# Strassen's seven products in the second MLP matmul of a Griffin-style block

## The chip, the cores and the metric

One core of a Trainium2 chip runs the kernel. The metric is the device time of one execution in microseconds (us). Engines are named as the profile names them: PE is TensorE (PEld its weight loads), DVE is VectorE, ACT is ScalarE, POOL is GpSimd, SP is SyncE, whose queue (SPq) issues every DMA here.

## The reference

One hybrid decoder block on 512 positions of 1024 channels: a mixer (RG-LRU branch and differential attention, merged and projected) and then a channel part, which is where the change lies. Cut to that part:

```python
h2 = rms_norm(x) * (1.0 + scale2) + shift2          # 512 x 1024
ff = jnp.square(jax.nn.relu(h2 @ w_ff1[l])) @ w_ff2[l]   # 1024 -> 4096 -> 1024
x = x + gate2 * ff
```

`shift2`, `scale2`, `gate2` are three of the six modulation vectors `c_act @ w_ada + b_ada`.

## The kernel before

All is fp32. A product in full precision is made of three matmuls in the float32r type: each operand is split into a high part (a cast to float32r) and a low part (the remainder), and `mm3` adds high x high, high x low and low x high in PSUM. `load_w` brings a weight block of 128 x 1024 into one of three `w` buffers, ACT casts it to `wh` (two buffers), DVE subtracts to get `wl` (two buffers). `project` multiplies such a block with all eight 128-row chunks of an activation: 8 x 3 = 24 matmuls of 512 columns, which give 128 output channels by 512 positions; I call this a block.

The MLP goes over four quarters `qd` of the 4096 hidden channels. In each, eight blocks of the first product (`project(w_ff1[qd, n], h2)`, tiles `f`) are passed through relu (ACT), squared (DVE), and split into `rh` (ACT) and `rlo` (DVE). Then eight blocks of the second product run over the quarter's 1024 hidden channels, and DVE adds each, scaled by `gate2`, to the residual `x1[n]` (line 867). In quarter 0 one `ada_chunk(5, n)` stands behind each of these blocks: it loads 128 x 1024 of `w_ada` into a `w` buffer and DVE reduces it to a column of `gate2` (line 183). In the last block of all, the 512 positions are done as two halves of 256 columns, so that the first half's store runs beside the second half. The first two blocks of quarter 0 (`early`, tiles `f1e`) are computed ahead, from the activation that is not yet normalised.

What is queued on each engine is set by a scheduler at build time, which may move independent instructions past one another; `tc.high_priority` lets the weight splits go ahead. At run time every engine takes its instructions in that order.

```python
wh, wl = load_w(src)
for k in range(KC):
    c0 = slice(k * P, (k + 1) * P)
    mm3(ps, wh[:, c0], wl[:, c0], act[k][0], act[k][1], k == 0, k == KC - 1)
```

Of the kernel before, what the change touches and what calls it, by code (L numbers as in the profile page):

```python
# [42 lines left out]
HP = 130  # L43
# [10 lines left out]
def build(tc, out, x, xT_in, c, pos, vecs, reps, ada, w_xr, w_xr7, w_qk, w_v, w_gr, w_gm, w_lru,  # L54
          w_pr, w_pa, w_out, w_ff1, w_ff2):
    nc = tc.nc
    from contextlib import ExitStack

    with ExitStack() as es:
        const = es.enter_context(tc.tile_pool(name="const", bufs=1))  # L60
        wpool = es.enter_context(tc.tile_pool(name="w", bufs=3))
        big = es.enter_context(tc.tile_pool(name="big", bufs=1))
        tmp = es.enter_context(tc.tile_pool(name="tmp", bufs=1))
        psum = es.enter_context(tc.tile_pool(name="ps", bufs=1, space=bass.MemoryType.PSUM))

        B_Q, B_Y, B_M, B_H, B_V, B_T, B_A, B_R = 12, 24, 8, 16, 8, 4, 6, 5

        def slot(tag, bufs, name, dt=F32):
            return big.tile([P, S], dt, name=name, tag=tag, bufs=bufs)

        def t_(name, dt=F32, tag="t"):
            return tmp.tile([P, S], dt, name=name, tag=tag, bufs=dict(t=B_T, a=B_A, r=B_R)[tag])

        def tiny(name, n, dt=F32):
            return tmp.tile([P, n], dt, name=name, tag=f"s{n}", bufs=4 if n >= 32 else 12)
# [1 line left out]
        def bank(name, tag="mm", bufs=4, dt=F32):  # L77
            return psum.tile([P, S], dt, name=name, tag=tag, bufs=bufs)
# [25 lines left out]
        def f32(t):  # L104
            return t.bitcast(F32)
# [4 lines left out]
        def load_w(src, n=1024):  # L110
            u = n_unit[0]
            n_unit[0] += 1
            w = wpool.tile([P, 1024], F32, name=f"w{u}", tag="w", bufs=3)
            nc.sync.dma_start(w[:, :n], src)
            wh = wpool.tile([P, 1024], F32R, name=f"wh{u}", tag="wh", bufs=2)
            wl = wpool.tile([P, 1024], F32R, name=f"wl{u}", tag="wl", bufs=2)
            with tc.high_priority(HP):
                i_w = nc.scalar.copy(wh[:, :n], w[:, :n])  # L118
                nc.vector.tensor_tensor(wl[:, :n], w[:, :n], f32(wh)[:, :n], op=ALU.subtract)  # L119
            last_wh[0] = i_w  # L120
            return wh, wl

        def mm3(ps, lh, ll, rh, rl, first, last):
            nc.tensor.matmul(ps, lh, rh, start=first, stop=False)  # L124
            nc.tensor.matmul(ps, lh, rl, start=False, stop=False)  # L125
            nc.tensor.matmul(ps, ll, rh, start=False, stop=last)  # L126

        def project(src, act, name):

            wh, wl = load_w(src)  # L130
            ps = bank(name)
# [3 lines that stand above are left out]
            return ps  # L135

        def split_l(dst, src, h):
            return nc.vector.tensor_tensor(dst, src, f32(h), op=ALU.subtract)  # L138


        c_sb = [t_(f"c_sb{i}") for i in range(2)]
        for i in range(2):
            nc.sync.dma_start(c_sb[i][0:1, :], c[:, i * S:(i + 1) * S])
        xt = [[slot("y", B_Y, f"x{i}_{j}") for j in range(2)] for i in range(TB)]
        for i in range(TB):
            for j in range(2):
# [8 lines left out]
        ident = const.tile([P, P], F32, name="ident")  # L155
# [45 lines left out]
        def mcol(j, k):  # L201
            return mod[:, j * 8 + k:j * 8 + k + 1]
# [30 lines left out]
        def bcast_cols(src, name, *where):  # L233

            dg = t_(name + "d")
            nc.vector.tensor_tensor(dg.rearrange("p (a b) -> p a b", b=P),
                                    ident[:, None, :].to_broadcast([P, TB, P]),
                                    src[:, :, None].to_broadcast([P, TB, P]), op=ALU.mult)
            pb = bank(name, *where)
            nc.tensor.matmul(pb, ones, dg, start=True, stop=True)  # L240
            return pb
# [19 lines left out]
        h = []  # L261
# [28 lines left out]
            return w  # L290

        nxt = first_chunk(0)
        rep = tmp.tile([P, 6, 64], F32, name="rep", tag="a", bufs=B_A)
        nc.sync.dma_start(rep, reps)
        pos_i = const.tile([P, TB], I32, name="pos_i")
        nc.sync.dma_start(pos_i, pos)
        for k in range(KC):
            wh, wl = nxt
            if k + 1 < KC:
                nxt = first_chunk(k + 1)  # L300
            for n in range(NK):
                c0 = slice(n * P, (n + 1) * P)
# [3 lines left out]
        def vtiny(name, n=8):  # L306
            return const.tile([P, n], F32, name=name)
# [13 lines left out]
        pl = vtiny("sp_p")  # L321
# [11 lines left out]
        for i in range(2):  # L333
            lj = t_(f"lj{i}")[:, :64]
            i_ = nc.vector.tensor_tensor_reduce(lj, rep[:, 2 + 2 * i], rep[:, 3 + 2 * i], 1.0, 0.0,
                                                op0=ALU.mult, op1=ALU.add, accum_out=lam2[:, i:i + 1])
# [13 lines left out]
        R = [P, TB, 32]  # L350

        def rtile(name):
            return tmp.tile(R, F32, name=name, tag="a", bufs=B_A)

        fr = rtile("fr")
        for i in range(32):
# [3 lines left out]
        kk = rtile("kk")  # L360
# [393 lines left out]
        for n in range(KC):  # L754
# [5 lines left out]
            mh = slot("y", B_Y, f"mh{n}", F32R)  # L760
# [7 lines left out]
        x1, hu = [], []  # L768
        acc = t_("acc", tag="a")
        for n in range(KC):  # L770
# [3 lines left out]
            t = slot("m", B_M, f"x1_{n}")  # L774
# [22 lines left out]
        rs2 = tiny("rs2", 4)  # L797
        rsqrt(rs2, pss[:, 0:2 * TB:2], 4, 1.0 / D, EPS, "r2")
        rb2p = bcast_cols(rs2, "rb2", "sc", 2)
        rb2 = t_("rb2s", tag="a")  # L800
        nc.scalar.copy(rb2, rb2p)


        NU = 2
        early = []
        pcs = bank("shift2w", "o", 1)
        for n in range(NU):
            wh, wl = load_w(w_ff1[0, n])
# [9 lines left out]
        shw = const.tile([P, NU], F32, name="shw")  # L818
        nc.vector.tensor_reduce(shw, pcs[:, :2 * NU].rearrange("p (a b) -> p a b", b=2), axis=AX.X, op=ALU.add)

        h2 = []
        for k in range(KC):
            t = t_(f"h2f{k}")
# [5 lines left out]
            h2.append((hh, hl))  # L829


        for qd in range(4):
            r2_ = []
            for n in range(KC):
                rl = t_(f"rl{qd}_{n}")
                if qd == 0 and n < NU:
                    nc.vector.tensor_tensor(rl, early[n], rb2, op=ALU.mult)
                    nc.scalar.activation(rl, rl, AF.Relu, bias=shw[:, n:n + 1])
                else:
                    ps = project(w_ff1[qd, n], h2, f"f1_{qd}_{n}")  # L840
                    nc.scalar.activation(rl, ps, AF.Relu)
                nc.vector.tensor_tensor(rl, rl, rl, op=ALU.mult)
                i = 2 * n
                tags = [("y", B_Y)] * 2 if qd % 2 == 1 else [("q", B_Q) if i + j < 12 else ("v", B_V) for j in (0, 1)]
                rh = slot(*tags[0], f"rh{qd}_{n}", F32R)
                nc.scalar.copy(rh, rl)
                rlo = slot(*tags[1], f"rlo{qd}_{n}", F32R)
                split_l(rlo, rl, rh)
                r2_.append((rh, rlo))
            for n in range(KC):  # L850
                if qd == 3 and n == KC - 1:

                    wh, wl = load_w(w_ff2[qd, n])
                    for hf in range(2):
                        cols = slice(hf * 256, hf * 256 + 256)
                        ps = bank(f"f2_{qd}_{n}_{hf}")[:, :256]
                        for k in range(KC):
                            c0 = slice(k * P, (k + 1) * P)
                            mm3(ps, wh[:, c0], wl[:, c0], r2_[k][0][:, cols], r2_[k][1][:, cols], k == 0, k == KC - 1)
                        nc.vector.scalar_tensor_tensor(x1[n][:, cols], ps, mcol(5, n), x1[n][:, cols],  # L860
                                                       op0=ALU.mult, op1=ALU.add)
                        nc.sync.dma_start(out[n][:, cols], x1[n][:, cols])
                    continue
                ps = project(w_ff2[qd, n], r2_, f"f2_{qd}_{n}")
                if qd == 0:
                    ada_chunk(5, n)
                nc.vector.scalar_tensor_tensor(x1[n], ps, mcol(5, n), x1[n], op0=ALU.mult, op1=ALU.add)  # L867
                if qd == 3:
                    nc.sync.dma_start(out[n], x1[n])


# [64 lines left out]
```

## Time and profile before

| what | value |
|---|---|
| runs: median (lowest to highest) | 906.08 us (905.87 to 906.85) |
| the profiled execution: its time | 905.49 us |
| the profiled execution: its span, first to last instruction | 903.7 us |
| busy in the span: PE, DVE, ACT | 98%, 63%, 43% |
| mean granted TensorE clock | 0.999 |
| chain that ended last: PE, DVE, DMA | 78%, 12%, 4% |

The page tells for each engine how much of the span it was busy, in 40 slices how that was spread, and who waited for whom. Matmuls are pipelined, so a matmul's shown length is not the time that it takes from the next; the starts tell that. An engine that idles costs nothing as long as PE does not wait for it.

### The profile page before, as it was taken

Reading aid. Unit: us, or ns where it says so; the run is one execution under the profiler, and the core shown is the slowest. Engines: PE = TensorE matmul, PEld = TensorE weight load, DVE = VectorE, ACT = ScalarE, POOL = GpSimd, SP = SyncE. Lnnn points to the kernel's source line nnn. Section 1 sums busy time; section 2 is a strip of 40 time slices with the busy share of each in tenths; the row PEclk is TensorE's granted clock in tenths of the full one; section 3 lists DMA queues with packets and bytes.
Section 4 is the critical chain, followed back from the end, with each engine's and each line's share of the span. In section 5 each row is a group of like instructions: output and inputs, shape, how many; then the busy total and the mean of one; then the engine's idle time right before and its main releaser. Section 6 shows DMA issues by size and latency. Waiting matters only on the chain.

```text
span 903.7 us, 11146 instructions
## 1 busy us (share of the span) xinstructions
PE 883.1 (98%) x4076; PEld 720.1 (80%) x4076; DVE 570.8 (63%) x1144; ACT 390.1 (43%) x676; POOL 2.2 (0%) x40
## 2 busy tenths in 40 slices
PE   6999999999999999999999999999999999999998
PEld 3888887777878878787778888888888888888887
DVE  6963974599969775987867566865344334334442
ACT  6663545985446444435533343531242133223420
POOL 0000000000000000000000000000000000000000
PEclk9999999999999999999999999999999999999999
DMA  8943226222263673367546332355222223322241
GB/s 321 343 144 105 94 101 156 102 70 71 76 156 121 178 217 120 137 165 226 203 144 206 117 105 71 100 183 200 99 94 94 94 94 99 110 94 94 93 140 47
DMA packets 42154, 121.57 MB, mean 135 GB/s; under 512 B 5618, under 2 KB 6002, under 8 KB 42100
## 3 DMA queue, kind: packets, MB, share of 16 engines
q1 hardware_dynamic: 42100, 120.87, 41.8%
q8 instruction: 32, 0.52, 0.2%
q14 instruction: 22, 0.18, 0.1%
HBM read 106.17 MB, written 2.10 MB: 120 GB/s over the span
## 4 chain that ended last, share of the span: by engine, by line
PE 78%; DVE 12%; DMA 4%; ACT 2%; issue 2%; SPq 2%; ACTq 0%; DVEq 0%
PE f L126 12%; PE f L124 12%; PE f L125 12%; DMA ada<-in_ada 3%; DVE wl L119 3%; PE xr L124 2%; PE xr L126 2%; PE xr L125 2%; PE wo L126 2%; PE wo L124 2%; PE gr L126 2%; PE gr L124 2%; PE wo L125 2%; PE gr L125 2%; PE qk L126 2%
## 5 line engine op out<-in xcount | busy, mean ns | idle before, releaser
L118 ACT CAST wh<-w 128x1024 fp32r<-128x1024 f32 (+1 forms) x145 | 151.6, 1046 | 330.6 <-PE f L125 176.8
L119 DVE TENSOR_TENSOR wl<-w,wh 128x1024 fp32r<-128x1024 f32 (+1 forms) x145 | 176.3, 1216 | 114.6 <-ACT wh L118 110.1
L125 PE MATMUL f<-rlo,wh 128*128 128x512 f32 (+1 forms) x264 | 101.1, 383 | 0.0
L126 PE MATMUL f<-rh,wl 128*128 128x512 f32 (+1 forms) x264 | 101.0, 383 | 0.0
L124 PE MATMUL f<-rh,wh 128*128 128x512 f32 (+1 forms) x264 | 101.0, 383 | 0.0
L126 PE MATMUL f<-h2h,wl 128*128 128x512 f32 x240 | 93.3, 390 | 0.1
L124 PE MATMUL f<-h2h,wh 128*128 128x512 f32 x240 | 93.2, 390 | 0.0
L125 PE MATMUL f<-h2l,wh 128*128 128x512 f32 x240 | 92.7, 389 | 0.0
L867 DVE SCALAR_TENSOR_TENSOR x<-f,mod,x 128x512 f32<-128x512 f32 x31 | 23.3, 751 | 86.7 <-PE f L126 86.7
L125 PEld LDWEIGHTS f<-rlo,wh 128*128 128x128 f32 x264 | 49.6, 188 | 10.0 <-DVE rlo L138 0.3
L124 PEld LDWEIGHTS f<-rh,wh 128*128 128x128 f32 x264 | 49.6, 188 | 9.7
L126 PEld LDWEIGHTS f<-rh,wl 128*128 128x128 f32 x264 | 49.6, 188 | 9.7
L126 PEld LDWEIGHTS f<-h2h,wl 128*128 128x128 f32 x240 | 45.0, 188 | 10.0 <-DVE wl L119 0.6
L183 DVE CUSTOM_DVE_ANT_0 ada<-ada,cb,bada 128x1024 f32<-128x1024 f32 x32 | 41.0, 1282 | 18.9 <-DMA ada<-in_ada 18.7
L125 PEld LDWEIGHTS f<-h2l,wh 128*128 128x128 f32 x240 | 45.0, 188 | 9.4
L124 PEld LDWEIGHTS f<-h2h,wh 128*128 128x128 f32 x240 | 45.1, 188 | 9.2
L126 PE MATMUL gm<-hh,wl 128*128 128x512 f32 x128 | 51.0, 399 | 0.0
L124 PE MATMUL gm<-hh,wh 128*128 128x512 f32 x128 | 50.8, 397 | 0.0
L124 PE MATMUL qk<-wh,hh 128*128 128x512 f32 x128 | 50.7, 398 | 0.0
L125 PE MATMUL gm<-hl,wh 128*128 128x512 f32 x128 | 50.7, 396 | 0.0
L126 PE MATMUL qk<-wh,hl 128*128 128x512 f32 x128 | 50.6, 395 | 0.0
L125 PE MATMUL qk<-wl,hh 128*128 128x512 f32 x128 | 50.3, 393 | 0.0
(314 smaller groups left out, 1734.8 us busy)
## 6 DMA issues: line engine op xcount, KB each, us to landing
w<-in_w_ff SPq DMA_DIRECT2D x64, 512.0 KB, 3.2
ada<-in_ada SPq DMA_DIRECT2D x32, 512.0 KB, 4.3
ada<-in_ada SPq DMA_DIRECT2D x32, 256.0 KB, 5.8
w<-in_w_qk SPq DMA_DIRECT2D x16, 512.0 KB, 3.3
w<-in_w_gm SPq DMA_DIRECT2D x16, 512.0 KB, 3.7
w<-in_w_gr SPq DMA_DIRECT2D x8, 512.0 KB, 3.3
w<-in_w_v SPq DMA_DIRECT2D x8, 512.0 KB, 3.2
kh<-qh SPq DMA_DIRECT2D x32, 128.0 KB, 2.4
```

The lines of the kernel that those rows point to most:

```text
L118: i_w = nc.scalar.copy(wh[:, :n], w[:, :n])
L119: nc.vector.tensor_tensor(wl[:, :n], w[:, :n], f32(wh)[:, :n], op=ALU.subtract)
L124: nc.tensor.matmul(ps, lh, rh, start=first, stop=False)
L125: nc.tensor.matmul(ps, lh, rl, start=False, stop=False)
L126: nc.tensor.matmul(ps, ll, rh, start=False, stop=last)
L183: nc.vector.tensor_tensor_reduce(w, w, cb, 1.0, bada[:, col:col + 1], op0=ALU.mult, op1=ALU.add, accum_out=mod[:, col:col + 1])
L867: nc.vector.scalar_tensor_tensor(x1[n], ps, mcol(5, n), x1[n], op0=ALU.mult, op1=ALU.add)
```

## The change

The quarter's second product is written with the positions as rows: activations A (512 positions x 1024 hidden, cut in halves A11, A12, A21, A22) times weights B (1024 hidden x 1024 outputs, cut in halves), by Strassen's scheme in Winograd's form, seven products of halves in place of eight. One product of halves is 2 row tiles x 4 hidden chunks x 3 = 24 matmuls, with a split activation chunk as the stationary operand and 512 output channels as the moving one.

- The squared activations stay unsplit in `raw` (ACT squares, no longer DVE). Sums of halves of A are made on DVE in `sx`, and each operand is split just before its product (`split_a`).
- B is loaded in eight tiles per quarter (`b`, in pieces of 1 KB); DVE forms sums of B tiles in place (`sums`); each operand is cast and subtracted in two halves (`split_b`), with two buffers for each half.
- The seven products go p1, p5, p6, p3, p7, p2, p4 (in quarter 3: p1, p2, p5, p6, p3, p7, p4). They accumulate in PSUM banks X, Z and Y, and after each DVE adds the bank to C in SBUF (`add_c`; the first time ACT copies it).
- In quarters 0 to 2 three blocks of the next quarter's first product (`beside`) run before p1, after p5 and after p6.
- At the end, `finish` transposes C with 32 transposes on PE and DVE adds it to `x1`; the last product is computed the other way round, in 48 matmuls of 256 columns, and needs no transpose.
- The eight `ada_chunk(5, n)` of quarter 0 stand together behind the first product's eight blocks.
- The buffers of the mixer come from a pool `mix`, closed before the MLP, whose memory the pool `ff` takes over.

```diff
-            for n in range(KC):
-                rl = t_(f"rl{qd}_{n}")
...
-                nc.vector.tensor_tensor(rl, rl, rl, op=ALU.mult)
...
-                ps = project(w_ff2[qd, n], r2_, f"f2_{qd}_{n}")
-                if qd == 0:
-                    ada_chunk(5, n)
-                nc.vector.scalar_tensor_tensor(x1[n], ps, mcol(5, n), x1[n], op0=ALU.mult, op1=ALU.add)
...
+        mix_es.close()
+        ff = es.enter_context(tc.tile_pool(name="ff", bufs=1))
...
+                    for hf in range(2):
+                        b = ff.tile([P, 4, 2 * P], F32, name=f"b{qd}_{k}{c}{hf}", tag="b", bufs=8)
+                        k0 = (4 * k + 2 * hf) * P
+                        nc.sync.dma_start(b, w_ff2[qd, 4 * c:4 * c + 4, :, k0:k0 + 2 * P].rearrange("n p f -> p n f"))
...
+                with tc.high_priority(HP):
+                    nc.scalar.copy(v4(wh), v)
+                    nc.vector.tensor_tensor(v4(wl), v, f32(v4(wh)), op=ALU.subtract)
...
+                        nc.vector.tensor_tensor(dst, dst, ps[t], op=ALU.add if sign > 0 else ALU.subtract)
...
+                fs = [split_b(b, f"{name}_{qd}_{i}", i) for i, b in enumerate(bs)]
+                for hf in range(2):
+                    for t in range(2):
+                        for kk in range(2):
+                            k = 2 * hf + kk
+                            ts = slice(t * P, (t + 1) * P)
+                            mm3(ps[t], a[0][:, k, ts], a[1][:, k, ts], fs[hf][0][:, kk], fs[hf][1][:, kk],
+                                first and k == 0, k == 3, not first)
...
+            if qd == 3:
+                second()
+            b12 = get_b(0, 1)
+            sums(b11, b12)
+            Z = [bank(f"Z{qd}_{t}") for t in range(2)]
+            product("p5", s1, b11, Z, True)
+            beside()
+            with tc.high_priority(HP):
+                nc.vector.tensor_tensor(sx, sx, A[0][0], op=ALU.subtract)
+                s2 = split_a(sx, "s2")
+            add_c(1, 1, Z, 1)
+            b22 = get_b(1, 1)
+            sums(b11, b22)
+            product("p6", s2, b11, X, False)
+            beside()
...
+            raw = hidden(qd, ahead)
+            if qd == 0:
+                for n in range(KC):
+                    ada_chunk(5, n)
...
+            beside()
+            out_product(qd, raw, beside)
```

Where the instructions then stand, at two places. First DVE around the end of quarter 0's hidden blocks (`wl` is a weight subtraction, `ada` a reduction, `a11l`, `s1l` low parts of activations, `p_0_1l` the low part of p1's second weights). Before:

```order
L119 TENSOR_TENSOR wl_5764<-w_5761,wh_5763 128x1024
L842 TENSOR_TENSOR rl_6_5685<-rl_6_5685 128x512
L138 TENSOR_TENSOR rlo_6_5721<-rl_6_5685,rh_6_5719 128x512
L119 TENSOR_TENSOR wl_5799<-w_5796,wh_5798 128x1024
L842 TENSOR_TENSOR rl_7_5723<-rl_7_5723 128x512
L183 ISA ada_5862,mod<-ada_5862,cb,bada 128x1024
L183 ISA mod 128x1
L138 TENSOR_TENSOR rlo_7_5759<-rl_7_5723,rh_7_5757 128x512
L867 SCALAR_TENSOR_TENSOR x_0_5035<-f_0_0_5767,mod,x_0_5035 128x512
L119 TENSOR_TENSOR wl_5834<-w_5831,wh_5833 128x1024
```

Now:

```order
L188 ISA ada_5753,mod<-ada_5753,cb,bada 128x1024
L188 ISA mod 128x1
L188 ISA ada_5756,mod<-ada_5756,cb,bada 128x1024
L188 ISA mod 128x1
L188 ISA ada_5759,mod<-ada_5759,cb,bada 128x1024
L188 ISA mod 128x1
L957 TENSOR_TENSOR sx_5839<-r_0_0_5532,r_0_1_5533 128x512
L123 TENSOR_TENSOR wl_5766<-w_5763,wh_5765 128x1024
L905 TENSOR_TENSOR p_0_1l<-b_001_5799,p_0_1h 128x1024
L143 TENSOR_TENSOR s1l_5843<-sx_5839,s1h_5842 128x512
```

A reduction between two weight subtractions was one of a pair before; now the subtraction for the first block of quarter 1 (`wl_5766`) stands behind all eight reductions, and its load stands behind their loads on SP.

Then DVE in quarter 3, from the splits for p6 to the addition that frees Z for p3 (`p_3_0l`, `p_3_1l` low parts of weights, `s4l` of an activation sum, `C` the accumulators). Before, at this place of quarter 3:

```order
L119 TENSOR_TENSOR wl_7534<-w_7531,wh_7533 128x1024
L867 SCALAR_TENSOR_TENSOR x_1_5075<-f_3_1_7504,mod,x_1_5075 128x512
L119 TENSOR_TENSOR wl_7567<-w_7564,wh_7566 128x1024
L867 SCALAR_TENSOR_TENSOR x_2_5117<-f_3_2_7537,mod,x_2_5117 128x512
L119 TENSOR_TENSOR wl_7600<-w_7597,wh_7599 128x1024
```

Now:

```order
L905 TENSOR_TENSOR p_3_1l<-b_111_7643,p_3_1h 128x1024
L948 TENSOR_TENSOR b_000_7495<-b_000_7495,b_100_7556 128x1024
L948 TENSOR_TENSOR b_001_7497<-b_001_7497,b_101_7558 128x1024
L905 TENSOR_TENSOR p_3_0l<-b_010_7594,p_3_0h 128x1024
L918 TENSOR_TENSOR C_5524<-C_5524,Y_0_7554 128x512
L905 TENSOR_TENSOR p_3_1l<-b_011_7596,p_3_1h 128x1024
L918 TENSOR_TENSOR C_5525<-C_5525,Y_1_7555 128x512
L918 TENSOR_TENSOR C_5530<-C_5530,Z_0_7600 128x512
```

One subtraction and one addition per block have become a row of sums, splits and additions, with the additions that free Y and Z behind the splits for later products.

## Rows read from the trace of the kernel before

**Rows 1.** The page: busy time of each engine, then tenths in 40 slices.
```profile
PE 883.1 (98%) x4076; PEld 720.1 (80%) x4076; DVE 570.8 (63%) x1144; ACT 390.1 (43%) x676; POOL 2.2 (0%) x40
...
DVE  6963974599969775987867566865344334334442
```
**Rows 2.** Windows over quarter 1: stretch, length, busy time by engine, granted clock, DMA.
```profile
638.70:682.20 43.50, 43.50 (x193) 36.04 (x192) 19.62 (x23) 16.23 (x22) 0.00 (x0) 1.00 0.29 97
682.20:725.70 43.50, 43.50 (x193) 36.03 (x192) 16.36 (x17) 9.55 (x10) 0.00 (x0) 1.00 0.28 97
```
**Rows 3.** Timeline of PE at the end: start, duration, instruction.
```profile
889.17 0.39 PE L124 MATMUL f<-rh,wh 128*128 128x512 f32 x1
...
894.61 0.28 PE L124 MATMUL f<-rh,wh 128*128 128x256 f32 x1
894.72 0.28 PE L125 MATMUL f<-rlo,wh 128*128 128x256 f32 x1
...
900.24 0.28 PE L126 MATMUL f<-rh,wl 128*128 128x256 f32 x1
```
**Rows 4.** Waits: engine, line, for whom; us in total, times, longest.
```profile
ACT wh L118 <- PE f L125: 176.8, 57, 4.4
DVE wl L119 <- ACT wh L118: 110.1, 56, 4.6
```
**Rows 5.** Transposes on PE: timeline in the attention stage, and their group.
```profile
427.90 0.60 PE L598 MATMUL aT<-ident,e 128*128 128x128 f32 x4
428.25 0.48 PE L124 MATMUL gm<-hh,wh 128*128 128x512 f32 x1
428.57 0.39 PE L125 MATMUL gm<-hl,wh 128*128 128x512 f32 x1
...
L598 PE MATMUL aT<-ident,e 128*128 128x128 f32 x80 | 14.2, 276 | 2.2 <-DVE yal L640 1.8 <-DVE or0b L94 0.2
```
**Rows 6.** Timeline of DVE where operations follow each other without a gap.
```profile
563.16 1.23 DVE L119 TENSOR_TENSOR wl<-w,wh 128x1024 fp32r<-128x1024 f32 x1 [0.19 <-ACT wh L118]
564.30 0.75 DVE L828 SCALAR_TENSOR_TENSOR h2l<-h2f,mod,h2h 128x512 fp32r<-128x512 f32 x1
...
568.93 0.69 DVE L837 TENSOR_TENSOR rl<-f1e,rb2s 128x512 f32<-128x512 f32 x1
569.53 0.74 DVE L828 SCALAR_TENSOR_TENSOR h2l<-h2f,mod,h2h 128x512 fp32r<-128x512 f32 x1
```
**Rows 7.** Timeline at hidden block 4 of quarter 0 (ACT, DVE, PE).
```profile
571.38 1.05 ACT L118 CAST wh<-w 128x1024 fp32r<-128x1024 f32 x1 [0.94 <-PE f L125]
...
572.47 1.23 DVE L119 TENSOR_TENSOR wl<-w,wh 128x1024 fp32r<-128x1024 f32 x1 [0.99 <-ACT wh L118]
...
573.75 0.50 PE L126 MATMUL f<-h2h,wl 128*128 128x512 f32 x1
574.09 0.39 PE L124 MATMUL f<-h2h,wh 128*128 128x512 f32 x1
```
**Rows 8.** The tile `ada` in quarter 0: reductions (ns) and loads.
```profile
L183 DVE CUSTOM_DVE_ANT_0 ada<-ada,cb,bada x8: 1284/1285/1286, 584.4 to 625.7; 128x1024 f32<-128x1024 f32 x8
...
DMA to landing us min/median/max: 3.4/4.3/4.6
```
**Rows 9.** Timeline of DVE: the last read of PSUM.
```profile
900.56 0.48 DVE L860 SCALAR_TENSOR_TENSOR x<-f,mod,x 128x256 f32<-128x256 f32 x1 [2.39 <-PE f L126]
```
**Rows 10.** DMA from 14 to 38 us in 40 slices; then stores in 1 KB pieces.
```profile
GB/s 362 389 382 388 404 410 377 377 386 396 411 406 383 388 386 386 405 393 406 380 392 389 386 388 404 382 406 379 386 399 397 395 378 366 386 392 417 389 382 395
...
out_dram<-x SPq DMA_DIRECT2D x2, 128.0 KB, 1.7
```
**Rows 11.** A window with PE half idle, and PE's longest wait.
```profile
420.00:425.00 5.00, 2.92 (x18) 2.32 (x19) 4.34 (x9) 5.00 (x11) 0.00 (x0) 1.00 0.44 161
...
PEld warm L217 <- DMA x<-in_x: 6.3, 1, 6.3
```

More of the change, by code (lines that the diff above doesn't have):

```diff
@@ L64, in build @@
         psum = es.enter_context(tc.tile_pool(name="ps", bufs=1, space=bass.MemoryType.PSUM))
+        mix_es = ExitStack()
+        mix = mix_es.enter_context(tc.tile_pool(name="mix", bufs=1))
         B_Q, B_Y, B_M, B_H, B_V, B_T, B_A, B_R = 12, 24, 8, 16, 8, 4, 6, 5
         def slot(tag, bufs, name, dt=F32):
-            return big.tile([P, S], dt, name=name, tag=tag, bufs=bufs)
+            return (big if tag in "mh" else mix).tile([P, S], dt, name=name, tag=tag, bufs=bufs)
         def t_(name, dt=F32, tag="t"):
-            return tmp.tile([P, S], dt, name=name, tag=tag, bufs=dict(t=B_T, a=B_A, r=B_R)[tag])
+            return (tmp if tag == "t" else mix).tile([P, S], dt, name=name, tag=tag,
+                                                     bufs=dict(t=B_T, a=B_A, r=B_R)[tag])
         def tiny(name, n, dt=F32):
@@ L121, in load_w, with mm3 @@
             return wh, wl
[L123 to L126, printed above, removed]
+        def mm3(ps, lh, ll, rh, rl, first, last, more=False):
+            nc.tensor.matmul(ps, lh, rh, start=first, stop=False, skip_group_check=more)
+            nc.tensor.matmul(ps, lh, rl, start=False, stop=False, skip_group_check=more)
+            nc.tensor.matmul(ps, ll, rh, start=False, stop=last, skip_group_check=more)
         def project(src, act, name):
@@ L292, in build @@
         nxt = first_chunk(0)
-        rep = tmp.tile([P, 6, 64], F32, name="rep", tag="a", bufs=B_A)
+        rep = mix.tile([P, 6, 64], F32, name="rep", tag="a", bufs=B_A)
         nc.sync.dma_start(rep, reps)
@@ L352, in rtile @@
         def rtile(name):
-            return tmp.tile(R, F32, name=name, tag="a", bufs=B_A)
+            return mix.tile(R, F32, name=name, tag="a", bufs=B_A)
         fr = rtile("fr")
@@ L799, in build @@
         rb2p = bcast_cols(rs2, "rb2", "sc", 2)
-        rb2 = t_("rb2s", tag="a")
+        rb2 = t_("rb2s")
         nc.scalar.copy(rb2, rb2p)
@@ L829, in build @@
             h2.append((hh, hl))
-        for qd in range(4):
-            r2_ = []
-            for n in range(KC):
-                rl = t_(f"rl{qd}_{n}")
[L836 to L841, printed above, removed]
-                nc.vector.tensor_tensor(rl, rl, rl, op=ALU.mult)
[L843 to L863, printed above, removed]
-                ps = project(w_ff2[qd, n], r2_, f"f2_{qd}_{n}")
-                if qd == 0:
-                    ada_chunk(5, n)
-                nc.vector.scalar_tensor_tensor(x1[n], ps, mcol(5, n), x1[n], op0=ALU.mult, op1=ALU.add)
-                if qd == 3:
-                    nc.sync.dma_start(out[n], x1[n])
@@ new lines, in build, with hidden_relu @@
+        mix_es.close()
+        ff = es.enter_context(tc.tile_pool(name="ff", bufs=1))
+        C = [[[ff.tile([P, S], F32, name=f"C{r}{c}{t}", tag="c", bufs=8) for t in range(2)]
+              for c in range(2)] for r in range(2)]
+        H2 = S // 2
+        def hidden_relu(qd, n, dst):
+            if qd == 0 and n < NU:
+                nc.vector.tensor_tensor(dst, early[n], rb2, op=ALU.mult)
+                nc.scalar.activation(dst, dst, AF.Relu, bias=shw[:, n:n + 1])
+            else:
+                ps = project(w_ff1[qd, n], h2, f"f1_{qd}_{n}")
+                nc.scalar.activation(dst, ps, AF.Relu)
@@ new lines, in build, with finish @@
+        n_fin = [0]
+        def finish(n, t0, t1, store=True):
+            pt = bank(f"cT{n}_{t0}", *(("tp", 1), ("o", 1))[n_fin[0] % 2])
+            n_fin[0] += 1
+            for t in range(t0, t1):
+                nc.tensor.transpose(pt[:, t * P:(t + 1) * P], C[t // 2][n // 4][t % 2][:, n % 4 * P:(n % 4 + 1) * P],
+                                    ident)
+            cols = slice(t0 * P, t1 * P)
+            nc.vector.scalar_tensor_tensor(x1[n][:, cols], pt[:, cols], mcol(5, n), x1[n][:, cols],
+                                           op0=ALU.mult, op1=ALU.add)
+            if store:
+                nc.sync.dma_start(out[n][:, cols], x1[n][:, cols])
@@ L873, in layout, with beside @@
+        ahead = []
+        for qd in range(4):
+            raw = hidden(qd, ahead)
+            if qd == 0:
+                for n in range(KC):
+                    ada_chunk(5, n)
+            ahead = []
+            def beside():
+                if qd < 3:
+                    ahead.append(t_(f"ahead{qd + 1}_{len(ahead)}"))
+                    hidden_relu(qd + 1, len(ahead) - 1, ahead[-1])
+            beside()
+            out_product(qd, raw, beside)
 def layout(inputs):
```

103 lines of the change are left out of this document (added).

## The prediction

> **What bounds the kernel now.** I read the page's busy shares and its 40 slices first. TensorE (PE) is busy 98% of the span, VectorE (DVE) 63%, ScalarE (ACT) 43%, and DVE's digits fall to 3 and 4 in the last third, where the MLP runs [rows 1]. Next the windows over the MLP: in the first product of quarter 1 PE is busy 43.50 us of 43.50 and DVE 19.62, in its second 43.50 and 16.36 [rows 2]. So PE bounds the whole MLP, and the order of its matmuls in the timeline gives the price: 24 of them (one block) from 889.17 to 894.61, 5.44 us, which is 0.2267 us each; the last 48, of 256 columns, start 0.12 us apart [rows 3]. The 0.39 us shown for each is its whole passage; they overlap. DVE and ACT mostly wait for PE here, as the waits say: 176.8 us of ACT's weight casts behind PE, 110.1 us of DVE's subtractions behind ACT [rows 4]. Fewer matmuls are therefore time gained, as long as DVE, which takes over the sums, stays ahead.
>
> **PE's work.** Seven products of 24 matmuls replace eight blocks of 24 in each of four quarters: 4 x 24 = 96 fewer, x 0.2267 = **-21.8 us**. (The last product of all stays in 48 pieces of 256 columns, as the last block was.) Added are 32 transposes of C. The trace has such transposes in fours: four start at 427.90, the next matmul at 428.25 and the one after at 428.57, so four cost 0.35 + 0.32 - 0.23 = 0.44 us [rows 5], 0.11 each, **+3.5 us** for 32. Their mean duration is 276 ns [rows 5]. The Trainium skill (TensorE: Matmul & The Clock Gate, Part 4: PE-mode transpose) counts about 275 ns for one in a kernel's context; if that were the slot it takes, 32 would be +8.8 us. The trace agrees with that as a duration and not as a slot, so the 0.11 stands.
>
> **DVE's work.** Back to back, an operation of 1024 columns starts 1.14 us before the next (563.16 to 564.30), one of 512 with PSUM or SBUF 0.60 (568.93 to 569.53), though they last 1.23 and 0.69 [rows 6]. A quarter's products cost DVE 14 weight splits, 8 sums of weights, 7 splits and 4 sums of activations, 14 additions to C. Where two hidden blocks run among the products (quarters 0 to 2), I count in the order 26 wide and 15 half operations between the start of the first product and the end of the seventh: 26 x 1.14 + 15 x 0.60 = 38.6 us, beside 9 x 5.44 = 49.0 us of PE. The cover is thus PE itself. Walking the queue in order, the tightest place is the weight subtraction of the second block run among the products, done 1 to 2 us before PE wants it. So quarters 1 and 2 cost **0**, bounded by nothing and 2 us each (a cast and a subtraction late: 1.05 + 1.14 [rows 6, 7]). ACT takes the squares from DVE and stays under its share; nothing of it is on the path.
>
> **Quarter 0.** The eight reductions `ada_chunk(5, n)` stood one behind each block of the second product; now they stand together, and all their loads share the three `w` buffers with the load for the first block of quarter 1, which stands behind them on the DMA queue of SP. The last subtraction ahead of the chain (weights of hidden block 6) I place at 582.1: block 4's own subtraction starts at 572.47 and its third matmul at 573.75 as before, a wide cast lasts 1.05 [rows 7]; ACT then has eight entries, 5.4 us, up to the cast for p5's first weights, done at 577.9; after it DVE has three wide operations and a half one ahead of that subtraction's end, 577.9 + 3 x 1.14 + 0.60 + 0.2 for the two hand-overs. From there: a load, a reduction, a load, a reduction, two more reductions, then the load of the weights and their cast. With L for a load: 582.1 + 2 x (L + 1.28) + 2 x 1.28 + L + 1.05 = 588.3 + 3L. L was 3.4 to 4.6 us for these loads, the reduction 1.28 [rows 8]: 598.5 to 602.1. PE needs it after hidden block 7 and the first twelve matmuls of p1: block 4's fourth matmul starts at 574.09 [rows 7], plus 21 x 0.2267 + 3 x 5.44 + 12 x 0.2267 = 597.9. So PE idles 0.6 to 4.2 us; the middle, **+2.4**. What waits behind on DVE (second half of p1's split) is late by the same and not more. The head of the MLP gets one cast of a B tile ahead of three of the casts to `h2h`, whose load cannot start before the last early matmul; I find its landing before ACT comes to it: 0, at most +1.
>
> **Quarter 3** has no hidden blocks among its products, so there DVE is the bound. Count from the end of hidden block 7 (t = 0): DVE's split of p2's second weights waits for ACT's cast, which waits for PE, so it starts at 1.1. Up to the addition that frees bank Z for p3 stand 17 wide and 8 half operations: 1.1 + 17 x 1.14 + 8 x 0.60 = 25.3, with 0.4 us for two short waits on ACT 25.7. PE has then done p1, p2, p5 and p6, 4 x 5.44 = 21.8, and waits 3.9 us, in which 4 transposes lie that are counted already: **+3.4**. With the full durations (1.23 and 0.69) it is 27.5 and 5.4 net; I take the paces, since those rows are back to back as here. p7 then just gets its operands (at 32.0, PE at 31.2 + four matmuls). Behind p7 the 28 transposes and the 48 matmuls of the last product alternate with DVE's reads of two banks: **+1.0**, between 0 and 2.5, from one 256-column read of 0.48 [rows 9] that stands between two transposes of a bank, two to five times. The tail (read, store) is the same as before.
>
> **The loads** of B come in pieces of 1 KB where a `w` load had 4 KB. The nearest rows: loads in pieces of 2 and 3.5 KB ran at 362 to 417 GB/s, stores in 1 KB pieces of 128 KB landed in 1.7 us [rows 10]. In quarters 1 to 3 a B tile may load as soon as a split frees a buffer, about one per 3 us (175 GB/s), long before it is read. In quarter 0 four loads (2.1 MB) follow the subtraction for hidden block 3 and must have landed some 12 to 14 us later: about 175 to 215 GB/s. 0 by the rows, since they are above.
>
> **Sum.** -21.8 + 3.5 + 2.4 + 3.4 + 1.0 = **-11.5 us** on the profiled execution's 905.49: 894.0. The median of the runs shown, 906.08, is 0.6 above it: **894.6**. With all lower bounds -14.3, 891.8; with all upper ones (4.2, 5.4, 2.5, 2 x 2, 1) -1.2, 904.9.
>
> **Rivals.**
> A, *everything hidden*: the chain in quarter 0 and DVE's lead in quarter 3 turn out better than the walk, only transposes are left: -21.8 + 3.5 + 2 = -16.3, 889.8. For it: the waits were summed from rows that stood in other company; against: DVE's queue in quarter 3 is longer than PE's by the row durations whichever are used.
> B, *late loads*: pieces of 1 KB load at less than 175 GB/s. For: no load in such pieces is in the trace. Against: the 1 KB stores. One late tile of 2 to 3 us in quarter 0: 897.
> C, *hand-overs late in every quarter*: only two buffers per kind of split exist, so each split's cast waits for a PE product to end, and DVE's queue stands behind that. If in quarters 0 to 2 every second product (about 10 in all) starts 1 us late, the gain is 1.5 us and the time 904.6; that decides between faster and no change. For: a subtraction stands 2 us or less ahead of its use in the walk. Against: DVE's 38.6 us in 49.0.
> D, *slower*: PE's clock falls at the 3.9 us wait before p3 of quarter 3. From p3 on PE has p3, p7 (48 x 0.2267 = 10.9), 28 transposes (3.1) and 48 x 0.12 = 5.8, together 19.8 us; at the half level all of it takes 19.8 more: 914.4. It decides from 11.5 us of those on, that is if the lower level lasted for more than half of the stretch. Against it: the granted clock is 1.00, the 2.4 GHz level, in every window, also in those with PE busy 2.92 us of 5, and after the 6.3 us wait at the start [rows 11]. The Trainium skill (TensorE: Matmul & The Clock Gate, Why this matters for your kernels) warns that idle gaps between bursts of matmuls bring the lower clock back; by it D would be likely. The trace disagrees as far as its waits go.
>
> **Chances.** Forecast 0.62; A 0.07; B 0.06; C 0.17 (0.07 still faster, 0.07 the same, 0.03 slower); D 0.08. A difference of 0.2%, 1.8 us, is about what a measurement of this kernel can tell from no change. Faster by more: 0.62 + 0.07 + 0.06 + 0.07 = 0.82; the same 0.07; slower 0.03 + 0.08 = 0.11. The range takes the bounds and A's end: 889.5 to 904.5; outside lie D and the worse part of C.
>
> **What would show it.** PE with 96 matmuls fewer and 32 transposes more; a matmul pace of 0.2267 in the products too; PE idle of 1 to 4 us at about 598, released by DVE or ACT of the first weights of quarter 1; another of near 4 us in the last 30 us, released by DVE's additions to C; nearly none in quarters 1 and 2, where DVE is busy about 0.8 in the products. Wrong it would be with waits of PE for DVE's weight splits spread over quarters 1 and 2 (C), for B's loads (B), or a granted clock below 1.00 near the end (D).

## The result, and the profile of the changed kernel

The changed kernel takes 896.12 us (median of four, 894.77 to 896.98) against 905.98 (904.15 to 906.85) for the kernel before: ratio 0.9895, 95% interval 0.9881 to 0.9908, so 9.9 us faster. 894.6 was predicted, between 889.5 and 904.5. The profiled execution took 894.77 us, its span is 893.0, 10.7 less than before; 11.5 less was predicted for it.

The page answers to [rows 1]; PE has 96 matmuls fewer and 32 transposes more (4076 - 96 + 32 = 4012), and DVE is now busy through the last third:

```profile
PE 867.7 (97%) x4012; PEld 707.0 (79%) x4012; DVE 657.4 (74%) x1227; ACT 448.3 (50%) x748; POOL 2.2 (0%) x40
...
DVE  6972983499969855895868566879646883876597
```

Windows over quarter 1 (stretch, length, busy time of PE, PEld, DVE, ACT, POOL, granted clock, DMA share, GB/s), against [rows 2]. The first is the end of quarter 0's products and then, from 652.79, hidden blocks; the second is, from 685.43 on, most of quarter 1's seven products with two hidden blocks among them:

```profile
638.00:682.00 44.00, 44.00 (x195) 36.45 (x195) 23.38 (x24) 20.36 (x27) 0.00 (x0) 1.00 0.35 117
682.00:726.00 44.00, 44.00 (x195) 36.42 (x194) 38.06 (x41) 23.34 (x28) 0.00 (x0) 1.00 0.32 106
```

PE does not pause there, with DVE busy 38.06 us of 44.00, 0.86, in the second. The pace in the products is that of a block: p2 of quarter 3 starts at 848.63 and the product behind it at 854.07, 24 matmuls in 5.44 us.

```profile
848.63 0.39 PE L129 MATMUL Y<-p_0h,a12h 128*128 128x512 f32 x1
...
854.07 0.39 PE L129 MATMUL Z<-p_0h,s1h 128*128 128x512 f32 x1
```

PE's waits (engine, line, for whom; us in total, times, longest). Of those not in the kernel before, three rows matter:

```profile
PE cT L1017 <- DVE C L918: 2.6, 2, 1.3
PE f L129 <- ACT wh L122: 2.3, 1, 2.3
...
PE Z L129 <- DVE C L918: 0.3, 1, 0.3
```

The second is in quarter 0. In the timeline there, SP issues the weights' load behind the reductions' loads, the last reduction runs at 598.08, the cast comes when the load has landed, and PE stands from 598.49 (598.26 + 0.23) to 600.94. Ahead of that, the eight reductions by their tile:

```profile
L188 DVE CUSTOM_DVE_ANT_0 ada<-ada,cb,bada x8: 1276/1285/1286, 582.1 to 598.1; 128x1024 f32<-128x1024 f32 x8
```

```profile
595.73 6.77 SPq L118 DMA_DIRECT2D w<-in_w_ff  x4
...
598.08 1.29 DVE L188 CUSTOM_DVE_ANT_0 ada<-ada,cb,bada 128x1024 f32<-128x1024 f32 x1 [0.55 <-DMA ada<-in_ada]
598.26 0.39 PE L131 MATMUL X<-p_0h,a11l 128*128 128x512 f32 x1
...
599.84 1.05 ACT L122 CAST wh<-w 128x1024 fp32r<-128x1024 f32 x1 [2.61 <-DMA w<-in_w_ff]
...
600.94 0.50 PE L129 MATMUL f<-h2h,wh 128*128 128x512 f32 x1 [2.29 <-ACT wh L122]
```

The other two are in quarter 3. In the timeline of PE, p6's last matmul starts at 864.89 and p3's first at 868.96, with four transposes between; DVE is at the additions of Y and Z, which its queue has behind the splits:

```profile
864.89 0.39 PE L131 MATMUL X<-p_1h,s2l 128*128 128x512 f32 x1
866.49 0.44 PE L1017 MATMUL cT<-ident,C 128*128 128x128 f32 x2 [1.22 <-DVE C L918]
868.27 0.44 PE L1017 MATMUL cT<-ident,C 128*128 128x128 f32 x2 [1.34 <-DVE C L918]
868.96 0.47 PE L129 MATMUL Z<-p_0h,s4h 128*128 128x512 f32 x1 [0.25 <-DVE C L918]
```

```profile
866.39 1.23 DVE L905 TENSOR_TENSOR p_1l<-b,p_1h 128x1024 fp32r<-128x1024 f32 x1
867.53 0.68 DVE L918 TENSOR_TENSOR C<-C,Y 128x512 f32<-128x512 f32 x1
868.13 1.28 DVE L918 TENSOR_TENSOR C<-C,Z 128x512 f32<-128x512 f32 x2
```

At the end, 28 transposes and 48 matmuls of 256 columns lie between 880.22 and the last matmul's start; the span ends at 893.0 (in [rows 9] DVE's last read began at 900.56 of 903.7):

```profile
880.22 0.60 PE L1017 MATMUL cT<-ident,C 128*128 128x128 f32 x4
...
889.03 0.28 PE L131 MATMUL pl<-a22h,pl_1l 128*128 128x256 f32 x1
...
889.35 0.48 DVE L941 SCALAR_TENSOR_TENSOR x<-pl,mod,x 128x256 f32<-128x256 f32 x1 [0.64 <-PE pl L131]
```

### The profile page after: what moved, and what is told of

Its sections match the earlier page's. It is cut to its first block, busy times and chain, and to the rows that moved or that the text cites. A ratio compares the mean times of both kernels' runs of the same rounds, so it can differ in the third digit from the quotient of the medians.

```text
span 893.0 us, 11189 instructions
## 1 busy us (share of the span) xinstructions
PE 867.7 (97%) x4012; PEld 707.0 (79%) x4012; DVE 657.4 (74%) x1227; ACT 448.3 (50%) x748; POOL 2.2 (0%) x40
## 4 chain that ended last, share of the span: by engine, by line
PE 74%; DVE 16%; DMA 5%; ACT 2%; issue 2%; SPq 0%; DVEq 0%; ACTq 0%
PE f L129 5%; PE f L130 5%; PE f L131 5%; DMA ada<-in_ada 3%; DVE wl L123 3%; PE X L131 3%; PE X L130 3%; PE X L129 3%; PE qk L131 2%; PE qk L129 2%; PE qk L130 2%; PE xr L129 2%; PE xr L131 2%; PE xr L130 2%; PE wo L130 2%
## 5 line engine op out<-in xcount | busy, mean ns | idle before, releaser
L122 ACT CAST wh<-w 128x1024 fp32r<-128x1024 f32 (+1 forms) x113 | 117.9, 1043 | 214.6 <-issue 56.2
L123 DVE TENSOR_TENSOR wl<-w,wh 128x1024 fp32r<-128x1024 f32 (+1 forms) x113 | 137.0, 1213 | 87.7 <-ACT wh L122 86.6
L129 PE MATMUL f<-h2h,wh 128*128 128x512 f32 x240 | 93.0, 390 | 2.3 <-ACT wh L122 2.3
L129 PEld LDWEIGHTS f<-h2h,wh 128*128 128x128 f32 x240 | 45.1, 188 | 12.0 <-ACT wh L122 2.7
L129 PE MATMUL gm<-hh,wh 128*128 128x512 f32 x128 | 51.1, 399 | 0.0
L129 PE MATMUL qk<-wh,hh 128*128 128x512 f32 x128 | 50.8, 398 | 0.0
L588 ACT ACTIVATE e<-e,nm 128x128 f32<-128x128 f32 (+3 forms) x64 | 35.8, 561 | 28.7 <-DVE nm L586 28.4
L905 DVE TENSOR_TENSOR p_1l<-b,p_1h 128x1024 fp32r<-128x1024 f32 x27 | 33.0, 1223 | 21.8 <-ACT p_1h L904 21.8
L904 ACT CAST p_0h<-b 128x1024 fp32r<-128x1024 f32 x27 | 28.5, 1054 | 27.2 <-PE X L131 14.0
L904 ACT CAST p_1h<-b 128x1024 fp32r<-128x1024 f32 x27 | 28.3, 1050 | 27.3 <-PE f L130 24.5
L905 DVE TENSOR_TENSOR p_0l<-b,p_0h 128x1024 fp32r<-128x1024 f32 x27 | 33.0, 1222 | 11.7 <-ACT p_0h L904 11.6
L948 DVE TENSOR_TENSOR b<-b,b 128x1024 f32<-128x1024 f32 x32 | 38.7, 1220 | 0.1
L586 DVE CUSTOM_DVE_ANT_0 e<-sc,mask 128x128 f32<-128x128 f32 (+3 forms) x64 | 30.3, 486 | 10.4 <-PE sc L581 10.4
```

The lines of the kernel that those rows point to most:

```text
L129: nc.tensor.matmul(ps, lh, rh, start=first, stop=False, skip_group_check=more)
L586: nc.vector.tensor_tensor_reduce(e[:, :n], ps[m][:, :n], mask[:, S - n:], 1.0, 1e30, op0=ALU.add, op1=ALU.min, accum_out=nm)
L588: nc.scalar.activation(e[:, :n], e[:, :n], AF.Exp, bias=nm, scale=-1.0, accum_out=sums[:, m:m + 1])
L904: nc.scalar.copy(v4(wh), v)
L905: nc.vector.tensor_tensor(v4(wl), v, f32(v4(wh)), op=ALU.subtract)
L948: nc.vector.tensor_tensor(d, d, s_, op=ALU.add)
```

## The experiments

All times are medians; the kernel before took 905.2 to 906.0 us beside them. The theory was the prediction's: PE's work is the bound, plus two waits, one for loads (quarter 0) and one for DVE's queue (quarter 3). The rivals were that the waits only move, and that the clock is in it.

**The kernel again.** No edit.

> The changed kernel once more, unaltered. In its profiled execution the granted clock fell to 0.56 from 160 to 163.4 us, right behind a wait of PE of 2.06 us in the mixer that the kernel before has too, there with the clock at 1.00; its three other runs were 1.3 to 2.2 us longer at a mean clock of 0.993. Theory: whether the clock falls behind a wait of 2 us or more is chance, in both kernels; then this profile may show it at other such waits (near 160, 598, 865 us), each fall worth some 1.6 us where PE is the bound, and the time lies between 894.5 and 897.5. Rival: the new waits bring the fall regularly; then it stands in this profile behind both of them, and not only in the mixer.

896.12 us (892.05 to 898.22). In this profile the clock fell behind the wait of quarter 3, to 0.50, which is 1.2 GHz, and came back after some 3.5 us; windows of 1 us, then starts of PE:

```profile
868.00:869.00 1.00, 0.46 (x3) 0.25 (x3) 1.00 (x3) 0.00 (x0) 0.00 (x0) 1.00 0.00 0
869.00:870.00 1.00, 1.00 (x4) 0.83 (x5) 1.00 (x3) 0.00 (x0) 0.00 (x0) 0.85 0.06 16
870.00:871.00 1.00, 1.00 (x3) 0.79 (x3) 1.00 (x3) 0.00 (x0) 0.00 (x0) 0.50 0.00 0
...
873.00:874.00 1.00, 1.00 (x5) 0.81 (x5) 0.00 (x0) 0.35 (x1) 0.00 (x0) 0.94 0.79 262
```

```profile
870.22 0.63 PE L130 MATMUL Z<-p_0l,s4h 128*128 128x512 f32 x1
870.65 0.63 PE L131 MATMUL Z<-p_0h,s4l 128*128 128x512 f32 x1
```

Matmuls start 0.43 us apart instead of 0.2267. The span is 894.6, 1.6 longer than in the first profile, where the clock stayed at 1.00 at this place. It fell behind the mixer's wait in both profiles, behind quarter 0's in neither: the rival, which wanted it behind both new waits, falls. But chance is not all of it. Taken with the profiles of the versions below, the clock fell behind quarter 3's wait of this length in four of five (the first profile is the fifth) and behind quarter 0's, where it was 2.2 to 2.5 us, in two of five; at neither place did it fall in any profile in which that wait was removed or filled.

**Reductions elsewhere.** `ada_chunk` runs behind hidden blocks of quarters 1 and 2.

```diff
-            if qd == 0:
-                for n in range(KC):
-                    ada_chunk(5, n)
...
+                    if 1 <= qd <= 2 and n_ada[0] < KC:
+                        ada_chunk(5, n_ada[0])
+                        n_ada[0] += 1
```

> The eight reductions for gate2 go from quarter 0's end to behind hidden blocks of quarters 1 and 2. Theory (the loads share the three w buffers and stand ahead of the weights of quarter 1's first block): PE's wait of 2.29 us at 598.6 is gone and nothing takes its place, -2.3 to -2.8 us, 893.5. Rival 1: the wait only moves, to the second half of p1's split or to p5's operands: less than 1 us gained, 895.5 or more. Rival 2: the spread loads delay hidden blocks of quarter 1 and 2, where w buffers are shared in the same way: waits of PE for ACT's or DVE's split of weights there, time 896 or more.

892.40 us, ratio to before 0.9862 (0.9842 to 0.9883). The row `f L129 <- ACT wh` is gone and none came in its place; what is left in the MLP:

```profile
PE cT L1022 <- DVE C L923: 2.6, 2, 1.4
PE f L131 <- DVE wl L123: 0.4, 1, 0.4
PE Z L129 <- DVE C L923: 0.3, 1, 0.3
```

The theory holds. The medians differ by 3.7 where the wait was 2.3; the rest is within their scatter, or falls of the clock saved, which these runs can't tell apart.

**Sums ahead of the splits, quarter 3.** `e` holds b12 + b22 in four tiles that are free by then, so that no sum waits for the split before it.

```diff
+            if qd == 3:
+                b12, b22 = get_b(0, 1), get_b(1, 1)
...
+                            nc.vector.tensor_tensor(d[j], u[:, 2 * j:2 * j + 2], v[:, 2 * j:2 * j + 2], op=ALU.add)
+                sums(b12, b11)
...
-            sums(b11, get_b(1, 0))
+                sums(get_b(1, 0), b11)
```

> In quarter 3 alone the sums of B tiles are formed in another order, with one pair of extra tiles, so that those for p5, p6, p7 and the last product no longer wait for a split of the product before and can be made beside hidden blocks. Theory (DVE's queue is the bound of quarter 3's products): from the end of hidden block 7 to the addition that frees Z, DVE has 13 wide and 9 half operations in place of 17 and 8, 13 x 1.14 + 9 x 0.60 + 1.1 = 21.3 us against PE's 21.8, so the waits of 1.22, 1.34 and 0.25 us ahead of p3 go: -2.8 to -3.4 us, 893.0. Rival: it is the bank, not the queue: Z is freed by its addition only after p5, whatever DVE has done before; the wait stays over 2 us and the time over 895.

892.64 us, ratio 0.9856 (0.9833 to 0.9878), -3.5. Of the three rows only quarter 0's is left (1.4 us in this execution), and the clock was at 1.00 up to the last matmul. So it was the order of DVE's queue, and not the bank.

```profile
PE f L129 <- ACT wh L122: 1.4, 1, 1.4
```

**No cover.** The blocks behind p5 and p6 go back to the others.

```diff
             product("p5", s1, b11, Z, True)
-            beside()
...
             product("p6", s2, b11, X, False)
-            beside()
```

> The two blocks of the next quarter that ran behind p5 and behind p6 in quarters 0 to 2 go back to the other hidden blocks; the one ahead of p1 stays. The same matmuls in another order. Theory (their matmuls cover DVE's splits and sums): each of quarters 0 to 2 gets a wait as quarter 3 has it: from the end of the block ahead of p1, DVE has 14 wide and 4 half operations to the addition that frees Z, 1.1 + 14 x 1.14 + 4 x 0.60 = 19.5 us, PE has p1, p5 and p6, 16.3: 3.2 us each, +6 to +12 us in all, 902 to 908. Rival: DVE's lead from the hidden blocks carries it through; under 1 us per quarter, 896 to 899.

900.44 us, +4.3, between the two. The wait for Z appears in quarters 1 and 2, 1.7 us each, and not in quarter 0. The waits from 605 to 860 us:

```profile
PE Z L129 <- DVE C L918: 3.4, 2, 1.7
```

The mechanism is the theory's, its size half. That some of DVE's row, which I started at the end of the block ahead of p1, is done before is likely, and was not tried.

**Transposes twice.**

```diff
-            for t in range(t0, t1):
+            for t in [t for t in range(t0, t1) for _ in range(2)]:
```

> The changed kernel with each of the 32 transposes of C issued twice into the same place. Four of the 32 more fall into the wait ahead of p3 in quarter 3, 28 lie on PE's path at the end. Theory (a transpose takes a slot of 0.11 us): +3.1 us, 899 against 896.1 for the changed kernel. Rival (a transpose takes as long as its shown duration of 276 ns): 28 x 0.276 = +7.7 us, 904. The Trainium skill (TensorE: Matmul & The Clock Gate, Part 4: PE-mode transpose) has about 275 ns for one, by which the rival would hold.

898.72 us, +2.6. In the timeline, from the first of the 56 at the end to the last matmul's start there are 12.04 us, where the changed kernel has 8.81; 3.23 for 28 more is 0.115 each. The rival falls. In this profile the clock fell behind both new waits (last lines; granted clock third from the end).

```profile
881.31 1.03 PE L1017 MATMUL cT<-ident,C 128*128 128x128 f32 x8
...
893.35 0.28 PE L131 MATMUL pl<-a22h,pl_1l 128*128 128x256 f32 x1
```

```profile
600.00:605.00 5.00, 5.00 (x18) 3.96 (x18) 5.00 (x6) 2.12 (x3) 0.00 (x0) 0.74 0.52 171
870.00:875.00 5.00, 5.00 (x19) 4.02 (x18) 2.84 (x5) 1.87 (x2) 0.00 (x0) 0.77 0.16 52
```

**A longer wait, and the same wait filled.** First more additions of Z ahead of p3; then also matmuls that nobody reads.

```diff
+                for sign in (-1, 1, -1, 1):
+                    add_c(1, 1, Z, sign)
```

```diff
+                for i in range(34):
+                    nc.tensor.matmul(dm, s4[0][:, 0, :P], h2[0][0], start=True, stop=True)
```

> The changed kernel; in quarter 3 the two additions of bank Z are followed by eight more of 512 columns that subtract and add Z again, so p3 waits 8 x 0.60 = 4.8 us longer, and what is queued behind on DVE is later by as much. Theory (a longer wait costs itself, and a fall of the clock behind it lasts some 3.5 us as in the repeated run, 1.6 us): +4.8 us, 901; up to 903 where every execution has the fall. Rival (the clock stays at the lower level for as long as the prediction's case D supposed, to the end): up to 20 us more, 915 or over, with a granted clock near 0.5 over the last 20 us.

901.27 us (900.05 to 906.00), mean clocks of 0.989 to 0.994 in all eight executions. The theory's size holds for the median, three executions lie above its 903; the rival falls. Windows of the profiled one: the clock falls inside the wait, which lasts to 873.32, and is back at 878.8.

```profile
868.00:869.00 1.00, 0.29 (x2) 0.05 (x1) 1.00 (x3) 0.00 (x0) 0.00 (x0) 0.76 0.00 0
870.00:871.00 1.00, 0.00 (x0) 0.00 (x0) 1.00 (x3) 0.00 (x0) 0.00 (x0) 0.50 0.00 0
874.00:875.00 1.00, 1.00 (x4) 0.81 (x3) 1.00 (x3) 0.00 (x0) 0.00 (x0) 0.50 0.09 16
...
878.00:879.00 1.00, 1.00 (x4) 0.77 (x4) 1.00 (x2) 0.26 (x2) 0.00 (x0) 0.62 0.28 94
879.00:880.00 1.00, 1.00 (x6) 0.83 (x5) 0.62 (x2) 0.93 (x1) 0.00 (x0) 1.00 0.00 0
```

> The kernel with the longer wait ahead of p3; 34 matmuls of 512 columns, whose results nobody reads, now run on PE in that wait (34 x 0.2267 = 7.7 us, up to the addition that frees Z). In the eight executions without them the mean clock was 0.989 to 0.994, and in the trace the clock was at 0.50 from 868.8 us to 878.6, from inside the wait on. Theory (what brings the fall is that PE idles): the clock stays at 1.00 there, the mean clock goes to 0.996 or more, and the time to 899.5, 1.6 us and more below 901.3. Rival (the fall has to do with the end of quarter 3, not with idling): the fall stays, 901 or more.

899.62 us (898.38 to 900.58), mean clocks of 0.996 to 1.00. The same stretch with PE kept busy:

```profile
865.60 7.87 PE L991 MATMUL dm<-h2h,s4h 128*128 128x512 f32 x34
```

```profile
865.00:870.00 5.00, 5.00 (x24) 4.14 (x23) 5.00 (x7) 1.06 (x1) 0.00 (x0) 1.00 0.00 0
870.00:875.00 5.00, 4.62 (x23) 3.62 (x22) 5.00 (x10) 0.00 (x0) 0.00 (x0) 1.00 0.00 0
```

The two kernels differ in the matmuls that fill the wait, and with PE's idling the fall goes: 1.65 us by the medians (the kernel before took 906.02 and 905.86 us beside them).

**Both waits removed**, the first and second edit together.

> The spread reductions and the early sums together: both waits of PE are removed. Theory: the two gains add, as they lie in different quarters, -3.7 and -3.5 us against the changed kernel's 896.1: 889.0; mean clocks of 0.997 to 1.00 as in the kernel before, since only the mixer's waits are left. Rival: the gains share the clock's falls, which are drawn by chance; then less than 6 us, 890 or more.

890.28 us (888.05 to 890.44), ratio 0.9815 (0.9800 to 0.9831): 5.8 below the changed kernel's 896.12, where the single gains add up to 7.2. Its profiled execution has one wait of PE left in the MLP, for block 4's split in quarter 0, which the changed kernel has too:

```profile
PE f L131 <- DVE wl L123: 0.4, 1, 0.4
```

Both waits are gone. By its number the rival is met (less than 6 us, 890 or more), and two of the five executions have a mean clock of 0.995, where the theory expected 0.997 to 1.00: the gains overlap a little, falls at other places take some back, or the medians scatter by as much; the runs can't tell these apart.

**The end.** From the end of DVE's last read to the end of the span there are 2.66 us before, 3.17 in the changed kernel and 3.81 in the one with both waits removed (882.31 + 0.48 to 886.6). Three kernels went after it, all made from that one, whose last read is:

```profile
882.31 0.48 DVE L948 SCALAR_TENSOR_TENSOR x<-pl,mod,x 128x256 f32<-128x256 f32 x1 [0.17 <-PE pl L131]
```

> As the one with both, and the stores of the transposed part are issued from ACT's queue, so that SP has only those of the last product. In the changed kernel the stretch from the last matmul's start to the end of the span is 3.97 us, in the kernel before 3.46. Theory (the last store stands behind others in SP's queue): the stretch goes back to about 3.46 in the trace, -0.5 us, too little for the median to show by itself: 888.5. Rival: it is the traffic of the stores, whatever the queue: it stays near 3.97.

889.73 us; the read ends at 884.75, the span at 888.5: 3.75 where it was 3.81. Another queue changes next to nothing; the theory falls.

> The version with both waits removed, without the four stores of 256 KB at the end (rows 512 to 1023 of the output are not written). From the end of DVE's last read to the end of the span there were 3.81 us with them (2.66 in the kernel before), while the DMA engines moved 336 to 385 GB/s up to 884.1 us. Theory (the last store of 128 KB shares the DMA engines with these four): the stretch falls to 2.66, -1.1 us. Rival (it is the end of the program, whatever the stores): it stays over 3.5.

888.89 us; 2.55 (884.77 + 0.48 to 887.8). With the queue ruled out, it is the traffic: the DMA engines (last two columns: share, GB/s) are full with the four large stores when the last is issued. The kernel with both waits removed, then this one:

```profile
880.60:882.60 2.00, 1.68 (x15) 1.47 (x13) 1.83 (x4) 0.00 (x0) 0.00 (x0) 1.00 0.95 349
882.60:884.10 1.50, 0.00 (x0) 0.00 (x0) 0.20 (x1) 0.00 (x0) 0.00 (x0) 1.00 1.02 354
```

```profile
882.60:884.60 2.00, 2.00 (x19) 1.93 (x17) 1.91 (x4) 0.00 (x0) 0.00 (x0) 1.00 0.01 4
884.77 0.48 DVE L948 SCALAR_TENSOR_TENSOR x<-pl,mod,x 128x256 f32<-128x256 f32 x1 [0.16 <-PE pl L131]
```

The last edit puts the transposes with a store first:

```diff
-            for n in range(4):
-                finish(n, 2, 4, False)
             for n in range(4, KC):
                 finish(n, 0, 4)
+            for n in range(4):
+                finish(n, 2, 4, False)
```

> The version with both waits removed; of the transposes at the end, those of the lower 512 output channels, which go with the four stores of 256 KB, now stand ahead of those of the upper half of the positions of the first 512 channels, which have no store of their own. The same work in another order. Theory (the last store shares the DMA engines with the four large ones, 3.81 us from DVE's last read to the end against 2.55 without them): the four are issued about 3 us earlier and the stretch falls to between 2.6 and 3.1 us: -0.7 to -1.2 us, 889.3 against 890.3, near what the medians can tell. Rival (DVE's reads of the transposes, now later for the last product's blocks, delay the end): the time is the same or longer, and the last read starts more than 0.31 us behind the last matmul.

888.56 us (887.57 to 890.80), ratio 0.9819 (0.9804 to 0.9834). The last read starts 0.32 behind the last matmul (883.15), where it was 0.31, and the stretch is 2.85 us (883.95 to 886.8), as the theory had it:

```profile
883.47 0.48 DVE L948 SCALAR_TENSOR_TENSOR x<-pl,mod,x 128x256 f32<-128x256 f32 x1 [0.24 <-PE pl L131]
```

The ratio is that of the kernel with both waits removed, within their intervals: the trace shows the 0.96 us, the medians can't. All three complete versions without the two waits (889.73, 890.28 and 888.56 us) beat the kernel before and the changed one.

## Why the prediction was right

*PE's work*: right. 4 x 24 x 0.2267 = 21.8 us went; the pace in the products is the same. *Transposes*: 28 at the end cost 8.81 - 5.63 = 3.18 us over the 48 matmuls alone ([rows 3], 894.61 to 900.24), 0.114 each with all waiting among them, and doubling them gave 0.115. The slot of 0.11 holds. The Trainium skill's 275 ns (TensorE: Matmul & The Clock Gate, Part 4: PE-mode transpose) is again near the shown duration, on average 279 ns in this profile, and not the slot.

*Quarter 0*: 2.4 predicted, 2.45 measured (598.49 to 600.94). The chain was read right: the subtraction for block 6 is done at 582.1, as placed, and the first reduction starts there; then come three loads one behind the other, of 3.2 to 4.4 us. One link is other than walked: between them stand three reductions, a weight subtraction and a sum, not four reductions, which is about 0.5 us more.

*Quarter 3*: 3.4 predicted net of the transposes; 868.96 - 865.12 - 0.44 = 3.4, with p6's last matmul over at 864.89 + 0.23 = 865.12. Taking paces and not durations was right: the DVE rows above start 1.14 and 0.60 apart, though they show 1.23 and 0.68.

*Quarters 1 and 2*: no wait, as forecast; the cover is real, since without it 1.7 us come in each.

*The end, transposes and matmuls in turn with DVE's reads*: 1.0 predicted, about 0.1 measured (3.18 - 28 x 0.11). Mis-sized: DVE's reads alternate with matmuls of another bank, and PE hardly waits.

*"The tail (read, store) is the same as before"*: failed. It is 0.5 us longer, and the four large stores of the transposed rows are why; the run without them and the swapped order show it for the kernel with both waits removed, and no such run was made of the changed kernel itself.

*The head*, 0 with at most +1: 0.57 (hidden block 7's last matmul starts at 595.54 against 594.97). 0.35 of it was there before the MLP (the first hidden block starts at 562.32 against 561.97), 0.2 is the split of block 4. Some 0.5 more is lost in short gaps in p6, p7 and behind the waits.

On the profiled executions: -21.8 + 3.2 + 0.4 + 2.45 + 3.4 + 0.5 + 0.6 + 0.5 = -10.7. The large terms were right by their mechanism; that the sum is only 0.8 off is in part luck, since 1.6 us that the prediction put at nothing (tail, head, gaps) stand against 0.9 us too much for the end.

*Rivals*: A fell, both waits were there. B: the B tiles landed in 3.5 us (512 KB, median), no wait for them. (The prediction's rate for quarter 0's four loads is wrong by its own figures, 2.1 MB in 12 to 14 us being 150 to 175 GB/s and not 175 to 215; and its upper bound of 5.4 us for quarter 3 leaves out the 0.4 us of short waits on ACT. Neither changes the forecast.) C needed late hand-overs in quarters 0 to 2; there are none.

**D** was right in its mechanism and wrong in its size. The prediction's own sign for it, a granted clock below 1.00 near the end, is there in four of the five profiles with that wait, though not in the first. The clock returns after about 3.5 us, so that the fall costs 1.6 us and not 19.8. The prediction set "the trace disagrees" against the Trainium skill's warning (TensorE: Matmul & The Clock Gate, Why this matters for your kernels) that idle gaps bring the lower clock back. The runs agree with the warning. What misled me was that one profile showed 1.00 behind every wait [rows 11]; it was one draw.

The kernel before is slower too where its mean clock is lower: over 41 executions beside the experiments it took 904.2 us (median) with mean clock 1.000, 905.8 at 0.998 to 0.999, 906.7 at 0.996 to 0.997. The two executions of the changed kernel at 1.000 took 892.05 and 893.44, its eight others, at 0.993 to 0.998, 894.77 to 898.22. Without falls the gain is thus about 904.2 - 892.7 = 11.5, the sum predicted, though by two executions of the changed kernel only; in the medians, 1.6 us of it are given back. That a lower mean clock comes from falls behind waits was seen in the profiles of the changed kernel and its versions; the one profile of the kernel before has no fall.

## What to carry to other kernels

When PE gives up work to VectorE, walk VectorE's queue stage by stage with paces from back-to-back rows: its mean share (74%) says nothing about a stage without other matmuls to cover it. Look for what stands in a queue ahead of the one operation that frees a bank or a buffer, and for a load that gets behind others that share its buffers; both were repaired here by another order, the second with four more tiles. And price a wait at a little more than its length where TensorE's clock may fall behind it; one profile does not show whether it does.

## What was not expected of the hardware

- The granted clock fell to 0.50 behind a wait of 2.06 us in the mixer in one execution and stayed at 1.00 in another, with the same work around it. The window there in the profile of the kernel before, then in the changed kernel's:

```profile
160.00:165.00 5.00, 5.00 (x21) 3.67 (x21) 1.88 (x4) 4.25 (x9) 0.00 (x0) 1.00 0.67 254
160.00:165.00 5.00, 5.00 (x15) 3.86 (x15) 1.49 (x3) 3.94 (x8) 0.00 (x0) 0.66 0.65 260
```

  By the MLP that execution is only 0.35 us behind the kernel before. That does not show that later waits took the fall up: the mixer is the same in all versions of the changed kernel, and their first hidden block starts at 562.3 to 563.7 us in the five profiles with this fall alone before it, and at 560.4 to 561.7 in the four with none, on average 1.8 us earlier.
- With 5.0 us of waiting in one piece (behind the two shorter waits) all eight executions had a mean clock of 0.989 to 0.994, and in the profiled one the fall began before PE resumed.
- A store of 128 KB behind 1 MB of others ended up to 1.3 us later than without them (3.81, or 3.75 with these on ACT's queue, against 2.55 us).
